# One 512-column matmul for the weights' high part, down projections in two halves of output tiles, and biases written to DRAM once

## The chip, the cores and the metric

The kernel runs on one core of a Trainium2 chip. The metric is device time in microseconds (us) of one execution. The median of three runs of the kernel before is 1639.91 us (1635.03 to 1642.86).

A core has five engines that run their own instruction streams and meet through semaphores: TensorE (PE in the profile; PEld is its loading of weights), VectorE (DVE), ScalarE (ACT), GpSimd (POOL) and SyncE (SP), which here only issues the loads of the weights. Matmul results land in PSUM, in banks of 512 float32 per partition.

## The reference

The reference computes two transformer-like blocks in float32 on one sequence of T = 256 tokens of width D = 1024:

```
def first_block(x, mem, ...):
    mem_n = rmsnorm(mem, mem_norm)
    for l in range(2):
        x = x + 0.5 * swiglu(rmsnorm(x, ffn1_norm[l]), ffn1_w_gate[l], ffn1_w_up[l], ffn1_w_down[l])
        h = rmsnorm(x, mix_norm[l])
        x = x + (even_mixer if l == 0 else odd_mixer)(h, ...)
        x = x + memory_cross_attention(rmsnorm(x, xa_norm[l]), mem_n, ...)
        x = x + 0.5 * swiglu(rmsnorm(x, ffn2_norm[l]), ...)
    return rmsnorm(x, final_norm)
```

`swiglu` is `(silu(x @ w_gate) * (x @ w_up)) @ w_down` with an inner width of 2816 = 22 x 128. `even_mixer` puts a short convolution beside attention in a sliding window of 128 keys (8 heads); `odd_mixer` is causal attention (8 heads) over the whole sequence; both add to the logits a bias that depends on the distance of query and key alone (`rel_bias`, 32 buckets by 8 heads). The cross attention has four heads over a memory of 256 rows. The second block has a swiglu, a mixer of a depthwise convolution beside gated linear attention, another swiglu, and a per-layer embedding with a last norm. There are six swiglus in all.

## The kernel before, in words

**Layout.** Activations lie feature by token: `x` is eight tiles of [128 features, 256 tokens]. Weights come from DRAM in 517 units of [128, 1024] float32 (512 KB), packed on the host in the order of their use. `Builder.unit` (L172) loads one into one of five staging tiles, and `halves` (L151) splits it: ScalarE casts it to `whi` (fp32r, L155), VectorE subtracts to get `wlo` (L158). `wpool` holds eight such pairs. A unit is eight blocks of 128 x 128.

**Products.** Activations are split in the same way, into a high and a low part: `Norm` holds `hh` and `hl` for the normed `x` (`norm_pair`, L309), and `split` (L277) makes `ah` and `al` from an intermediate result. `mm3` (L222) multiplies one block of weights by an operand of 256 columns with three matmuls into the same 256 columns of a bank: high by high (L230), high by low (L231), low by high (L232). `proj` (L241) makes column tiles of a projection, two to a bank of the pool `psw` (four banks); `vproj` (L255) makes a projection by token, with 512 moving columns of weights (L271 to L273).

**Residual sums.** `accumulate` (L287) holds all eight output tiles of a down or output projection in the four banks of the pool `psa`, two tiles to a bank. Each row of weights (a unit: eight blocks) is added to all eight; the last `tail` rows are done pair by pair, and after each pair `updater` (L525) adds the bank to `x` (L530, or L532 with a factor), and `norm_pair` makes the next norm's operands from it (`hh` L316 on ScalarE, L314 on VectorE for the last pair; `hl` L317) and the squares (L328), summed on GpSimd (L336, L339). The norm's factor comes later: its reciprocal roots are spread over the partitions (`rb`) and multiplied into the results of the projection.

**Swiglu.** `ffn` (L401) projects gate and up of tile j into one bank, three tiles ahead (`LAG`) of the down product that uses them: VectorE multiplies the bank by `rb` (L408), ScalarE takes silu (L410), VectorE multiplies gate by up (L412), and `split` gives the operand (L282, L283). Operands live in the pool `act`, eight pairs. The first projection after a norm runs over the tiles of `x` in the outer loop (`kouter`), so that it can begin when the first tiles are normed.

**Attention.** `by_distance` (L599) makes the biases by distance, 8 heads by 384 distances, and writes each of two such tables to DRAM 128 times over (`fd`, [128, 8, 384], L605); `bias_tile` (L480) reads it back along diagonals into `tb`, 128 queries by 256 keys for four heads, which `softmax_block` (L433) adds to the scores (L445).

**Order.** The instructions are traced in program order, and a scheduler that plans with its own cost model orders them on each engine; at run time each engine's stream is in order. Some steps are put off by hand: `b.after` counts blocks of products, `b.bg` runs small steps with each unit of weights, and `HOLD`, `HOLD2` and `ASET` make the splitting of some units wait for a norm's last instructions. Tile pools that open in a stage reuse the memory of pools that have closed, and the first writer waits for the last reader.

The last mixer (`_gla_mixer`, L932) and the embedding at the end use the same helpers.

Of the kernel before, what the change touches and what calls it, by code (L numbers as in the profile page):

```python
# [19 lines left out]
P = 128  # L20
# [7 lines left out]
# swiglu tiles projected ahead of their use, and down tiles whose products end pair by pair  # L28
LAG, TAIL = 3, 3
# [19 lines left out]
# columns of the per-partition parameter array  # L49
# [15 lines left out]
class Norm:  # L65
    """Gained activations split in two, and the reciprocal root mean squares, which come later:
    `finish` gives them by token and a function that spreads them over the partitions."""

    def __init__(self, b, hh, hl, finish):
        self.b, self.hh, self.hl, self.finish = b, hh, hl, finish  # L70
        self.f32 = None
        self.sq = [None, None]
        self.state = 0
        self.gap = 12
        self.waiting = []

    def __call__(self, k):
        return self.hh[:, k, :], self.hl[:, k, :], self.f32 and self.f32[:, k, :]
# [43 lines left out]
class Builder:  # L122
    def __init__(self, ctx, tc, wflat):
# [7 lines left out]
        self.spread = self.square = None  # L131
        e = ctx.enter_context
        self.cpool = e(tc.tile_pool(name="cpool", bufs=1))
        self.stage = e(tc.tile_pool(name="stage", bufs=5))
        self.wpool = e(tc.tile_pool(name="wpool", bufs=8))
        self.work = e(tc.tile_pool(name="work", bufs=2))
        self.small = e(tc.tile_pool(name="small", bufs=4))
        self.act = e(tc.tile_pool(name="act", bufs=8))
# [33 lines left out]
    def unit(self, *slabs, raw=False):  # L172
        """The next 1024 columns of weights, split in two unless `raw`."""
# [10 lines left out]
    def first_units(self, specs, x, x_in, n, g):  # L184
        """The first two units and the input, in pieces that arrive together."""
# [36 lines left out]
    def mm3(self, ps, w, b, a, first, last):  # L222
        """One block of weights by an operand of 256 columns, each the sum of two exact parts."""
# [3 lines left out]
        if raw is not None:  # L227
            mm(ps, raw[:, s], a[2], start=first, stop=last, skip_group_check=True)  # L228
        else:
            mm(ps, hi[:, s], a[0], start=first, stop=False, skip_group_check=True)  # L230
            mm(ps, hi[:, s], a[1], start=False, stop=False, skip_group_check=True)  # L231
            mm(ps, lo[:, s], a[0], start=False, stop=last, skip_group_check=True)  # L232
# [8 lines left out]
    def proj(self, units, h, kouter=False, pool=None):  # L241
        """Column tiles of a projection, two to a bank."""
# [11 lines left out]

    def vproj(self, name, l, c0, h, raw=False):  # L255
        """Token-major projection onto 512 columns: two banks of 128 tokens."""
        banks = [self.psw.tile([P, 512], F32, tag="bank", name="bank") for _ in range(2)]
        mm = self.nc.tensor.matmul
        for u in range(ND // 2):
            hi, lo, w = self.vunit(name, l, u, c0, raw)  # L260
            for kk in range(2):
                k = 2 * u + kk
                ah, al, a = h(k)
# [12 lines left out]

    def split(self, src, name="a"):  # L277
        """A [128, 256] operand as two halves whose sum is exact."""
        nc = self.nc
        ah = self.act.tile([P, T], F32R, tag="ah", name="ah")  # L280
        al = self.act.tile([P, T], F32R, tag="al", name="al")
        nc.scalar.copy(ah, src)  # L282
        nc.vector.tensor_tensor(al, src, ah.bitcast(F32), op=ALU.subtract)  # L283
        return ah, al, None

# [1 line left out]
    def accumulate(self, parts, finish, tail=2):  # L287
        """parts: callables giving (weights, operand); finish(pair, bank)."""
# [15 lines left out]
    def norm_begin(self, finish=None):  # L304
        hh = self.hpool.tile([P, ND, T], F32R, tag="hh", name="hh")
        hl = self.hpool.tile([P, ND, T], F32R, tag="hl", name="hl")
        return Norm(self, hh, hl, finish or self.norm_end)

    def norm_pair(self, n, p, x, g, squares=True):  # L309
        """The operands from two tiles of x, [128, 8, 256], with gains g, [128, 8]."""  # L310
        nc = self.nc
        for d in (2 * p, 2 * p + 1):
            if p == 3:
                nc.vector.tensor_scalar_mul(n.hh[:, d, :], x[:, d, :], g[:, d:d + 1])  # L314
            else:
                nc.scalar.mul(n.hh[:, d, :], x[:, d, :], g[:, d:d + 1])  # L316
            self.last = nc.vector.scalar_tensor_tensor(n.hl[:, d, :], x[:, d, :], g[:, d:d + 1],  # L317
# [954 lines left out]
```

## Time and profile before

| | before |
|---|---|
| median of three runs | 1639.91 us (1635.03 to 1642.86) |
| profiled execution, span from first to last instruction | 1638.6 us |
| granted TensorE clock, mean | 0.987 |
| TensorE busy | 1597.3 us, 97%, 12606 matmuls |
| VectorE busy | 1079.8 us, 66% |
| ScalarE busy | 785.5 us, 48% |
| GpSimd busy | 108.2 us, 7% |
| DMA | 282.68 MB, mean 173 GB/s |

The profile gives no time of its own for the profiled execution beside its span. Engines work side by side, so the busy times don't add up. In a row of a group of instructions stand the line, the engine, the operation, what it writes and reads, the shape and the count; then the busy time and the mean of one; then the idle time of the engine before these instructions and what ended it. A matmul's duration includes the depth of its pipeline; matmuls start closer together than they last.

### The profile page before, as it was taken

What the parts mean: (1) busy time and instruction counts of PE and PEld (TensorE: products, weight loads), DVE (VectorE), ACT (ScalarE), POOL (GpSimd) and SP (SyncE); (2) the same over time, 40 slices, a digit from 0 to 9 for tenths busy, and PEclk for the clock granted to TensorE, in tenths of its full rate; (3) what the DMA queues carried; (4) which work ended last, traced back from release to release, by engine and by line L of the source; (5) the groups of instructions that cost most, each with busy time, mean ns of one, the idle gap of its engine ahead of it and who ended that gap; (6) DMA issues with size and microseconds to landing.
All of it is one profiled execution on the core that took longest, in us unless ns stands there. A gap on an engine that the chain in (4) does not pass through costs nothing. (4 is left out here: it accounts for less than half of the span.)

```text
span 1638.6 us, 30481 instructions
## 1 busy us (share of the span) xinstructions
PE 1597.3 (97%) x12606; PEld 1552.8 (95%) x12606; DVE 1079.8 (66%) x1552; ACT 785.5 (48%) x1201; POOL 108.2 (7%) x133
## 2 busy tenths in 40 slices
PE   8998899999999999999999999999999999999997
PEld 7998798989999999999999999999999978999996
DVE  6744578577656585556856865568555698756556
ACT  6432444355444454444644644454444666544444
POOL 4100010001000000001010100010000100200001
PEclk9999799999999999999999999999999999999999
DMA  7765745264655365553625655536555424665541
GB/s 267 229 165 133 217 169 170 91 206 155 210 186 184 129 231 182 184 186 119 218 78 181 208 191 180 182 115 231 184 187 184 150 84 132 208 205 183 181 142 65
DMA packets 78987, 282.68 MB, mean 173 GB/s; under 512 B 9450, under 2 KB 9722, under 8 KB 78848
## 3 DMA queue, kind: packets, MB, share of 16 engines
q1 hardware_dynamic: 75600, 272.66, 50.2%
q0 software_dynamic: 2672, 7.21, 2.6%
q8 instruction: 99, 1.62, 0.4%
q10 hardware_dynamic: 576, 0.86, 0.2%
q14 instruction: 40, 0.33, 0.1%
HBM read 276.49 MB, written 4.19 MB: 171 GB/s over the span
## 5 line engine op out<-in xcount | busy, mean ns | idle before, releaser
L158 DVE TENSOR_TENSOR wlo<-st,whi 128x1024 fp32r<-128x1024 f32 (+1 forms) x511 | 620.9, 1226 | 274.1 <-ACT whi L155 273.0
L155 ACT CAST whi<-st 128x1024 fp32r<-128x1024 f32 (+1 forms) x511 | 527.4, 1043 | 508.6 <-PE bank L231 331.5
L230 PE MATMUL bank<-hh,whi 128*128 128x256 f32 x2520 | 720.6, 286 | 16.4 <-ACT whi L155 14.7
L232 PE MATMUL bank<-hh,wlo 128*128 128x256 f32 x2520 | 718.5, 285 | 1.3 <-DVE wlo L158 0.9
L231 PE MATMUL bank<-hl,whi 128*128 128x256 f32 x2520 | 718.2, 285 | 0.6 <-DVE hl L317 0.6
L230 PEld LDWEIGHTS bank<-hh,whi 128*128 128x128 f32 x2520 | 488.5, 194 | 19.0 <-ACT whi L155 15.2
L232 PEld LDWEIGHTS bank<-hh,wlo 128*128 128x128 f32 x2520 | 488.2, 194 | 3.0 <-DVE wlo L158 3.0
L231 PEld LDWEIGHTS bank<-hl,whi 128*128 128x128 f32 x2520 | 488.5, 194 | 1.2 <-DVE hl L317 0.8
L230 PE MATMUL abank<-ah,whi 128*128 128x256 f32 x1312 | 372.8, 285 | 1.9 <-ACT whi L155 1.9
L232 PE MATMUL abank<-ah,wlo 128*128 128x256 f32 x1312 | 372.2, 284 | 0.7 <-DVE wlo L158 0.7
L231 PE MATMUL abank<-al,whi 128*128 128x256 f32 x1312 | 372.3, 284 | 0.0
L230 PEld LDWEIGHTS abank<-ah,whi 128*128 128x128 f32 x1312 | 252.6, 193 | 2.9 <-ACT whi L155 2.1
L231 PEld LDWEIGHTS abank<-al,whi 128*128 128x128 f32 x1312 | 252.8, 193 | 1.8 <-issue 1.6
L232 PEld LDWEIGHTS abank<-ah,wlo 128*128 128x128 f32 x1312 | 252.6, 193 | 1.3 <-DVE wlo L158 1.0
L408 DVE TENSOR_TENSOR gu<-bank,rb 128x512 f32<-128x512 f32 x132 | 90.5, 689 | 82.2 <-PE bank L232 82.1
L282 ACT CAST ah<-a 128x256 fp32r<-128x256 f32 x132 | 53.0, 405 | 131.3 <-DVE a L412 131.1
L283 DVE TENSOR_TENSOR al<-a,ah 128x256 fp32r<-128x256 f32 x132 | 56.6, 433 | 52.2 <-ACT ah L282 52.1
L336 POOL TENSOR_TENSOR sqa<-sq 128x256 f32<-128x256 f32 x13 | 10.3, 794 | 1131.6 <-ACT sq L328 953.5
L410 ACT ACTIVATE sg<-gu 128x256 f32<-128x256 f32 x132 | 54.0, 413 | 46.4 <-DVE gu L408 46.3
L339 POOL TENSOR_TENSOR sqa<-sqa,sq 128x256 f32<-128x256 f32 x78 | 69.1, 886 | 35.2 <-ACT sq L328 31.0
L317 DVE SCALAR_TENSOR_TENSOR hl<-x,pc,hh 128x256 fp32r<-128x256 f32 x88 | 57.6, 694 | 12.1 <-ACT hh L316 12.1
L316 ACT ACTIVATE hh<-x,pc 128x256 fp32r<-128x256 f32 x66 | 29.9, 501 | 68.1 <-DVE x L530 41.9
(247 smaller groups left out, 966.6 us busy)
## 6 DMA issues: line engine op xcount, KB each, us to landing
st<-wflat SPq DMA_DIRECT2D x515, 512.0 KB, 4.2
fd<-fs POOLq DMA_DIRECT2D x2, 1536.0 KB, 37.5
tb<-fd POOLq DMA_DIRECT2D x4, 512.0 KB, 4.4
x<-x_in SPq DMA_DIRECT2D x4, 256.0 KB, 5.7
st<-wflat SPq DMA_DIRECT2D x4, 256.0 KB, 5.2
mem<-mem_in POOLq DMA_DIRECT2D x4, 256.0 KB, 8.8
gf<-last_gain POOLq DMA_DIRECT2D x1, 512.0 KB, 8.1
out_dram<-y ACTq DMA_DIRECT2D x2, 256.0 KB, 2.5
```

The source lines that it names most:

```text
L155: self.nc.scalar.copy(w[0][:, s], st[:, s])
L158: self.nc.vector.tensor_tensor(w[1][:, s], st[:, s], w[0][:, s].bitcast(F32), op=ALU.subtract)
L230: mm(ps, hi[:, s], a[0], start=first, stop=False, skip_group_check=True)
L231: mm(ps, hi[:, s], a[1], start=False, stop=False, skip_group_check=True)
L232: mm(ps, lo[:, s], a[0], start=False, stop=last, skip_group_check=True)
L282: nc.scalar.copy(ah, src)
L283: nc.vector.tensor_tensor(al, src, ah.bitcast(F32), op=ALU.subtract)
L316: nc.scalar.mul(n.hh[:, d, :], x[:, d, :], g[:, d:d + 1])
L317: self.last = nc.vector.scalar_tensor_tensor(n.hl[:, d, :], x[:, d, :], g[:, d:d + 1], n.hh[:, d, :].bitcast(F32), op0=ALU.mult, op1=ALU.s ...
L339: add(n.sq[which], n.sq[which], dst[:, e, :], op=ALU.add)
L408: nc.vector.tensor_tensor(gu, bank, self.rb2(n), op=ALU.mult)
L410: nc.scalar.activation(sg, gu[:, 0, :], AF.Silu)
```

## The change

**Operands.** High and low parts of an activation now lie next to each other: `Norm` holds one tile `h2` [128, 8, 2, 256], and `split` makes one tile `a2` [128, 2, 256]. The pool for `a2` is opened per stage (`acts`): 22 in a swiglu, 8 in a mixer, 4 in a cross attention, 2 in the embedding.

**Products.** `mmw` multiplies a block's `wlo` by the high part (256 columns) and its `whi` by both parts (512 columns) into a whole bank; the result is the sum of the bank's two halves. `projw` uses one bank per column tile; ScalarE copies one half out and VectorE adds the other, in a new tile `sum`, which the multiplication by `rb` then reads. It replaces `proj` in the swiglus, both mixers of the first block and the cross attentions. The last mixer keeps `proj`, `mm3`, `accumulate` and the old `updater`; `vproj` stays.

**Residual sums.** `accumulatew` does output tiles 0 to 3 first, row by row, in `psa`, and then 4 to 7 one after the other, in `psw`, each over all rows. `blocks` gives it weights in units of eight blocks in that order, so the number of units stays 517. `updaterw` adds both halves of a bank to `x` in two instructions per output tile, and makes the norm's operands tile by tile.

**Biases.** The tables are written once each ([8, 384]) with the distances in the opposite order; `bias_tile` reads them with a step of one element from partition to partition, and `softmax_block` reads `tb` backward.

**Buffers.** `wpool` has seven pairs in place of eight. `LAG` stays 3; `TAIL` goes.

```diff
+    def blocks(self, order):
+        for i in range(0, len(order), 8):
+            u = self.unit(*order[i:i + 8])
+            for c in range(len(order[i:i + 8])):
+                yield u, c
...
+    def mmw(self, bank, w, b, a, first, last):
+        hi, lo, _ = w
+        s = slice(b * P, (b + 1) * P)
+        a = a[0]
+        mm = self.nc.tensor.matmul
+        mm(bank[:, 0, :], lo[:, s], a[:, 0, :], start=first, stop=False, skip_group_check=True)
+        mm(bank, hi[:, s], a, start=False, stop=last, skip_group_check=True)
+        self.tick()
...
+    def projw(self, units, h, kouter=False):
+        banks = [None] * len(units)
+        sums = []
+        order = [(c, k) for c in range(len(units)) for k in range(ND)]
+        if kouter:
+            order.sort(key=lambda ck: ck[1])
+        for c, k in order:
+            if k == 0:
+                banks[c] = self.psw.tile([P, 2, T], F32, tag="bank", name="bank")
+            self.mmw(banks[c], units[c], k, h(k), first=(k == 0), last=(k == ND - 1))
+            if k == ND - 1:
+                if c % 2 == 0:
+                    sums.append(self.work.tile([P, 2, T], F32, tag="sum", name="sum", bufs=4))
+                dst = sums[-1][:, c % 2, :]
+                self.nc.scalar.copy(dst, banks[c][:, 1, :])
+                self.nc.vector.tensor_tensor(dst, banks[c][:, 0, :], dst, op=ALU.add)
+        return sums
...
+        a = self.act.tile([P, 2, T], F32R, tag="a2", name="a2")
+        nc.scalar.copy(a[:, 0, :], src)
+        nc.vector.tensor_tensor(a[:, 1, :], src, a[:, 0, :].bitcast(F32), op=ALU.subtract)
...
+    def accumulatew(self, name, l, rows, operand, finish):
+        n = len(rows)
+        cols = [slice(d * P, (d + 1) * P) for d in range(ND)]
+        order = [(name, l, r, cols[d]) for r in rows for d in range(4)]
+        blocks = self.blocks(order)
+        banks = None
+        for i in range(n):
+            a = operand(i)
+            if banks is None:
+                banks = [self.psa.tile([P, 2, T], F32, tag="abank", name="abank") for _ in range(4)]
+            for d in range(4):
+                self.mmw(banks[d], *next(blocks), a, first=(i == 0), last=(i == n - 1))
+                if i == n - 1:
+                    finish(d, banks[d])
+        blocks = self.blocks([(name, l, r, cols[d]) for d in range(4, ND) for r in rows])
+        for d in range(4, ND):
+            bank = self.psw.tile([P, 2, T], F32, tag="bank", name="bank")
+            for i in range(n):
+                self.mmw(bank, *next(blocks), operand(i), first=(i == 0), last=(i == n - 1))
+            finish(d, bank)
...
+    def updaterw(n, g, scale=1.0):
+        def f(d, bank):
+            for e in range(2):
+                nc.vector.scalar_tensor_tensor(x[:, d, :], bank[:, e, :], scale, x[:, d, :], op0=ALU.mult, op1=ALU.add)
+            b.norm_tile(n, d, x, g)
+            if d >= 6:
+                b.sq_tile(n, d, x)
+            elif d % 2:
+                b.sq_pair(n, d // 2, x, 0)
...
-        def act(j, bank):
-            gu = self.work.tile([P, 2, T], F32, tag="gu", name="gu")
-            nc.vector.tensor_tensor(gu, bank, self.rb2(n), op=ALU.mult)
+        def act(j, gu):
+            nc.vector.tensor_tensor(gu, gu, self.rb2(n), op=ALU.mult)
...
-        blocks = ((0, slice(0, P), slice(P, T)), (1, slice(P, 384), slice(0, T)))
+        blocks = ((0, slice(0, P), slice(P - 1, None, -1)), (1, slice(P, 384), slice(None, None, -1)))
...
-        src = bass.AP(tensor=f.tensor, offset=f.offset + 127 + 4 * g * 384, ap=[[3071, P], [384, 4], [1, T]])
+        src = bass.AP(tensor=f.tensor, offset=f.offset + 4 * g * 384, ap=[[1, P], [384, 4], [1, T]])
...
-                fd = b.dram.tile([P, 8, 384], F32, tag=f"fd{i}", name="fd")
-                nc.gpsimd.dma_start(fd.rearrange("q h u -> h q u"), fs.unsqueeze(1).to_broadcast([8, P, 384]))
+                fd = b.dram.tile([8, 384], F32, tag=f"fd{i}", name="fd")
+                nc.gpsimd.dma_start(fd, fs)
```

`norm_tile` is the body of `norm_pair` for one tile; `sq_tile` squares one tile and adds it to the sum.

More of the change, by code (lines that the diff above doesn't have):

```diff
@@ L27 @@
 N_UNITS = 517
-LAG, TAIL = 3, 3
+LAG = 3
 HOLD, HOLD2, ASET = 0b11000, 0b100000, 0b10000
@@ L77, in __call__ @@
     def __call__(self, k):
-        return self.hh[:, k, :], self.hl[:, k, :], self.f32 and self.f32[:, k, :]
+        return self.h2[:, k, :, :], self.f32 and self.f32[:, k, :]
     def close(self, wait=0, gap=None):
@@ L275, in vproj, with acts @@
         return banks
+    @contextmanager
+    def acts(self, n):
+        self.n_acts += 1
+        with self.tc.tile_pool(name=f"act{self.n_acts}", bufs=n) as self.act:
+            yield
     def split(self, src, name="a"):
         nc = self.nc
[L280 to L284, printed above, removed]
+        a = self.act.tile([P, 2, T], F32R, tag="a2", name="a2")
+        nc.scalar.copy(a[:, 0, :], src)
+        nc.vector.tensor_tensor(a[:, 1, :], src, a[:, 0, :].bitcast(F32), op=ALU.subtract)
+        return a, None
     def accumulate(self, parts, finish, tail=2):
@@ new lines, in norm_begin, with norm_tile @@
+    def norm_begin(self, finish=None):
+        h2 = self.hpool.tile([P, ND, 2, T], F32R, tag="h2", name="h2")
+        return Norm(self, h2, finish or self.norm_end)
+    def norm_tile(self, n, d, x, g):
+        nc = self.nc
+        hh, hl = n.h2[:, d, 0, :], n.h2[:, d, 1, :]
+        if d >= 6:
+            nc.vector.tensor_scalar_mul(hh, x[:, d, :], g[:, d:d + 1])
+        else:
+            nc.scalar.mul(hh, x[:, d, :], g[:, d:d + 1])
+        self.last = nc.vector.scalar_tensor_tensor(hl, x[:, d, :], g[:, d:d + 1], hh.bitcast(F32),
+                                                   op0=ALU.mult, op1=ALU.subtract)
+        self.since = 0
@@ L309, in norm_pair @@
     def norm_pair(self, n, p, x, g, squares=True):
-        nc = self.nc
         for d in (2 * p, 2 * p + 1):
[L313 to L317, printed above, removed]
-                                                       n.hh[:, d, :].bitcast(F32), op0=ALU.mult, op1=ALU.subtract)
-            self.since = 0
+            self.norm_tile(n, d, x, g)
@@ L398, in rb2, with ffn, swiglu @@
         return n.rb.unsqueeze(1).to_broadcast([P, w, T])
-    def ffn(self, n, gate, up, down, finish, first=None):
+    def ffn(self, n, *args, **kw):
+        with self.acts(NFF):
+            self.swiglu(n, *args, **kw)
+    def swiglu(self, n, gate, up, down, finish, first=None):
         nc = self.nc
@@ L419, in produce, with operand @@
             us = first(specs) if first and j == 0 else [self.unit(*sp) for sp in specs]
-            bank = self.proj(us, n, kouter=(j == 0))[0]
-            n.then(lambda: act(j, bank))
-        def part(j):
-            def f():
-                while nxt[0] < min(j + 1 + LAG, NFF):
-                    produce()
-                return self.rowunit(down[0], down[1], slice(j * P, (j + 1) * P)), acts[j]
-            return f
-        self.accumulate([part(j) for j in range(NFF)], finish, TAIL)
+            s = self.projw(us, n, kouter=(j == 0))[0]
+            n.then(lambda: act(j, s))
+        def operand(j):
+            while nxt[0] < min(j + 1 + LAG, NFF):
+                produce()
+            return acts[j]
+        self.accumulatew(*down, [slice(j * P, (j + 1) * P) for j in range(NFF)], operand, finish)
     def softmax_block(self, heads, score, tb, s, sink=None):
@@ L681, in even @@
                 for i in (0, 2):
-                    bank = b.proj([b.colunit("ev_w_in", 0, qcols[i + e]) for e in range(2)], n)[0]
+                    bank = b.projw([b.colunit("ev_w_in", 0, qcols[i + e]) for e in range(2)], n)[0]
                     nc.vector.scalar_tensor_tensor(q[:, i:i + 2, :], bank, 0.125, b.rb2(n), op0=ALU.mult, op1=ALU.mult)
@@ L746, in even @@
                 rows = [slice(i * P, (i + 1) * P) for i in range(4)] + _permuted_heads(512)
-                b.accumulate([(lambda i=i: (b.rowunit("ev_w_out", 0, rows[i]), ys[i])) for i in range(8)],
-                             updater(n2, mid("xa_norm", 0)))
+                b.accumulatew("ev_w_out", 0, rows, lambda i: ys[i], updaterw(n2, mid("xa_norm", 0)))
         def odd(n, n2):
-            with tc.tile_pool(name="od", bufs=1) as op:
+            with b.acts(8), tc.tile_pool(name="od", bufs=1) as op:
                 tb = b.bias_tile(op, 1, 0)
@@ L858, in products @@
             s = slice(t * P, (t + 1) * P)
-            mm(bank, h[0][:, s], w[0][:, c], start=first, stop=False)
-            mm(bank, h[0][:, s], w[1][:, c], start=False, stop=False)
-            mm(bank, h[1][:, s], w[0][:, c], start=False, stop=last)
+            ah, al = h[0][:, 0, s], h[0][:, 1, s]
+            mm(bank, ah, w[0][:, c], start=first, stop=False)
+            mm(bank, ah, w[1][:, c], start=False, stop=False)
+            mm(bank, al, w[0][:, c], start=False, stop=last)
             b.tick(2)
@@ L958, in conv_in @@
         def conv_in(i, bank):
-            t = b.work.tile([P, 2, T], F32, tag="gu", name="gu")
+            t = b.work.tile([P, 2, T], F32, tag="sum", bufs=4, name="gu")
             nc.vector.tensor_tensor(t, bank, b.rb2(n), op=ALU.mult)
```

88 lines of the change are left out of this document (44 added, 44 removed).

## The prediction

> **What bounds the kernel now.** I read the page's totals first, then the chain, then busy time by stage. In the stage rows the fields after the window are its length, then PE, PEld, DVE, ACT and POOL busy time with the number of instructions, the granted clock, the DMA share and GB/s.
>
> ```profile
> PE 1597.3 (97%) x12606; PEld 1552.8 (95%) x12606; DVE 1079.8 (66%) x1552; ACT 785.5 (48%) x1201; POOL 108.2 (7%) x133
> PE 29%; ACT 1%; DVE 1%; POOL 0%; issue 0%; DMA 0%; POOLq 0%; ACTq 0%; DVEq 0%
> 130.00:140.00 10.00, 10.00 (x86) 10.00 (x86) 4.34 (x11) 3.15 (x6) 0.73 (x1) 1.00 0.01 2
> 158.00:184.00 26.00, 14.17 (x67) 12.60 (x67) 5.57 (x6) 5.83 (x7) 0.00 (x0) 0.68 0.61 138
> 190.00:200.00 10.00, 10.00 (x86) 10.00 (x85) 8.00 (x12) 6.09 (x9) 0.00 (x0) 1.00 0.89 296
> 229.00:250.00 21.00, 19.95 (x158) 19.14 (x157) 19.43 (x29) 11.57 (x12) 3.73 (x5) 0.98 0.77 267
> 330.00:386.00 56.00, 54.85 (x383) 50.71 (x381) 38.41 (x60) 27.70 (x50) 5.89 (x9) 1.00 0.49 160
> 386.00:566.00 180.00, 179.86 (x1498) 179.54 (x1497) 113.46 (x137) 83.48 (x111) 2.07 (x3) 1.00 0.59 194
> ```
>
> TensorE sets the pace: it is busy 97% of the span, and in a swiglu (386 to 566 us) never idle, one matmul per 180 / 1498 = 0.120 us, while VectorE works 63% and ScalarE 46% of it. Two stages are different. From 158 to 184 us only 67 matmuls start; at 0.120 us they need 8.0 us, so 18.0 us are lost. From 229 to 250 us, the head of the first mixer, VectorE works 19.4 of 21 us.
>
> ```profile
> 165.34 1.04 ACT L155 CAST whi<-st 128x1024 fp32r<-128x1024 f32 x1 [18.42 <-DMA st<-wflat]
> 141.80 1.13 POOL L605 DMA_DIRECT2D fd<-fs  x1 [8.18 <-DVE fs L603]
> fd<-fs POOLq DMA_DIRECT2D x2, 1536.0 KB, 37.5
> tb<-fd POOLq DMA_DIRECT2D x4, 512.0 KB, 4.4
> 231.36 0.81 POOL L486 DMA_DIRECT2D tb<-fd  x1
> L445 DVE TENSOR_TENSOR s<-abank,tb x32: 277/352/416, 249.0 to 805.4; 128x128 f32<-128x128 f32 x16, 128x256 f32<-128x256 f32 x16
> st<-wflat SPq DMA_DIRECT2D x515, 512.0 KB, 4.2
> ```
>
> The lost time has its cause here: the second write of the biases (1.5 MB, issued at 141.8, 37.5 us to land, so until about 179) shares the DMA engines with the weights, and ScalarE waits 18.4 us for a unit.
>
> **Term 1, TensorE.** The stage before the end runs the split products with 512 and then with 256 moving columns, each matmul with its own weight load. First of the 512, first and last of the 256:
>
> ```profile
> 1619.71 0.39 PE L859 MATMUL bank<-whi,hh 128*128 128x512 f32 x1
> 1624.47 0.28 PE L859 MATMUL bank<-whi,hh 128*128 128x256 f32 x1
> 1630.10 0.28 PE L861 MATMUL bank<-whi,hl 128*128 128x256 f32 x1
> L230 PE MATMUL bank<-hh,whi 128*128 128x256 f32 x2520 | 720.6, 286 | 16.4 <-ACT whi L155 14.7 <-DVE rb L389 1.7
> L230 PE MATMUL abank<-ah,whi 128*128 128x256 f32 x1312 | 372.8, 285 | 1.9 <-ACT whi L155 1.9
> L230 PE MATMUL bank<-mh,whi 128*128 128x256 f32 x64 | 18.4, 288 | 0.0
> ```
>
> 21 starts lie between the first two rows: 4.76 / 21 = 0.2267 us. 47 lie between the last two: 5.63 / 47 = 0.1198 us. The busy mean of 285 ns is the pipeline's depth and not the price; the price is start to start, 13 ns plus 0.417 ns a column. A block of weights costs 3 x 0.120 = 0.360 us now and 0.120 + 0.2267 = 0.3467 us after: one fixed 13.3 ns is saved. There are 2520 + 1312 + 64 = 3896 blocks. The last mixer keeps the old form for 168 of them (13 units of eight and its 64 output blocks), so 3728 change: 3728 x 13.3 ns = **49.6 us**. The order 256 after 512 in one stream of pairs isn't shown but once (at 1624.47); bounds are no gain (0.360 stays) and 49.6, and I take 49.6, since both widths show the same fixed part.
>
> The Trainium skill, "TensorE: Matmul & The Clock Gate", section "Back-to-back issue gap", speaks against this: it gives an isolated gap of N/2.4 + 2.5 ns, by which a block would go from 327.5 to 325.0 ns and the whole gain would be 9.3 us. The rows give 119.8 and 226.7 where that rule has 109.2 and 215.8, so here a matmul with its load keeps about 13 ns of its own, and the sum goes by the rows.
>
> **Term 2, the biases.** The two writes of 1.5 MB become 12 KB each, and the weights have the engines to themselves. The stall at 158 us goes: **18.0 us**. Bounds: 0 (something else holds the weights back at that point) and 18.0; I take all, since the write's 141.8 to 179 us is where the weights are late. The reads `tb<-fd` keep their 512 KB in 512 rows of 1 KB, now from one 12 KB region; they are issued at 231 us and first used at 249, so 4.4 us may become four times as long at no cost. Weights: 512 KB per eight blocks is 189 GB/s, below the 296 of the row at 190 us.
>
> **Term 3, what the wide bank adds.** Each projected column tile gives two halves: ScalarE copies one out, VectorE adds the other. There are 264 such tiles in the swiglus, 18 in the first mixer, 12 in the second, 16 in the cross attentions: 310. Every residual update becomes two VectorE instructions per output tile where one served a pair.
>
> ```profile
> L158 DVE TENSOR_TENSOR wlo<-st,whi 128x1024 fp32r<-128x1024 f32 (+1 forms) x511 | 620.9, 1226 | 274.1 <-ACT whi L155 273.0
> L155 ACT CAST whi<-st 128x1024 fp32r<-128x1024 f32 (+1 forms) x511 | 527.4, 1043 | 508.6 <-PE bank L231 331.5 <-DMA st<-wflat 132.5 <-issue 15.9
> L408 DVE TENSOR_TENSOR gu<-bank,rb 128x512 f32<-128x512 f32 x132 | 90.5, 689 | 82.2 <-PE bank L232 82.1
> L412 DVE TENSOR_TENSOR a<-sg,gu 128x256 f32<-128x256 f32 x132 | 55.5, 424 | 9.6 <-ACT sg L410 9.6
> L283 DVE TENSOR_TENSOR al<-a,ah 128x256 fp32r<-128x256 f32 x132 | 56.6, 433 | 52.2 <-ACT ah L282 52.1
> L283 DVE TENSOR_TENSOR al<-bank,ah 128x256 fp32r<-128x256 f32 x20 | 8.4, 423 | 9.8 <-ACT ah L282 9.8
> L410 ACT ACTIVATE sg<-gu 128x256 f32<-128x256 f32 x132 | 54.0, 413 | 46.4 <-DVE gu L408 46.3
> L282 ACT CAST ah<-a 128x256 fp32r<-128x256 f32 x132 | 53.0, 405 | 131.3 <-DVE a L412 131.1
> L476 ACT COPY pt<-bank 128x256 f32<-128x256 f32 x16 | 5.5, 373 | 3.9 <-PE bank L475 3.9
> L532 DVE SCALAR_TENSOR_TENSOR x<-abank,x 128x512 f32<-128x512 f32 x24 | 16.5, 688 | 14.3 <-PE abank L232 14.2
> L317 DVE SCALAR_TENSOR_TENSOR hl<-x,pc,hh x88: 468/485/1034, 5.0 to 1602.5; 128x256 fp32r<-128x256 f32 x88
> L314 DVE TENSOR_SCALAR hh<-x,pc x22: 347/353/834, 10.7 to 1600.8; 128x256 fp32r<-128x256 f32 x22
> ```
>
> The copy is L476's 0.373 us, the add L283's from PSUM, 0.423: 116 us on ScalarE (785 to 901) and 131 on VectorE. The half-width update isn't shown; it lies between half of L532 (0.344) and L532 (0.688), and I take 0.423, the PSUM operation of its width. That is 8 x 2 x 0.423 - 4 x 0.688 = 4.0 us for each of ten residual sums, 40 in all: VectorE 1080 + 131 + 40 = 1251, 79% of the new span. What hides it is TensorE. Take a swiglu's first half, where a step is one gate and one up tile and four down blocks: 20 blocks x 0.3467 = 6.93 us. VectorE has 2.5 splits (3.07), two adds (0.85) and L408, L412, L283 (1.55): 5.46 us, 79%. ScalarE has 2.5 casts (2.61), two copies (0.75) and 0.82: 4.17 us. Both fit, and the 331.5 us that casts waited for matmuls to free a weight buffer say that units are split as early as the buffers allow; seven buffers are 19 us ahead, against 4.2 for a landing. The new wait is the add's for the copy: behind it on VectorE stand the multiplication by the norm and the next split, and TensorE misses that split only when the seven buffers are used up. A column tile now holds a whole bank of four, but it is wanted again only four tiles later, 11 us and more.
>
> Where the cover is thin:
> - The last operand of a swiglu is needed 12 blocks (4.2 us) after its projection, where its chain is 0.37 + 0.42 + 0.69 + 0.41 + 0.42 + 0.41 + 0.43 = 3.2 us clean, and may queue behind a split of 1.2. Between 0 and 1 us, six times; I take 0.5 each, **+3**.
> - The cross attention's output product has only four rows, 32 blocks, 11.1 us. Its first output tile is ready after 13 blocks (4.5 us); from there VectorE has eight tiles of two updates (0.85) and `hl` (0.48 to 1.03 by L317's spread; 0.74 taken), and two `hh`: 13.4 us, to 17.9. TensorE is through, with the 14 blocks of the next projection that need no eighth tile, at 11.1 + 4.9 = 16.0, and waits about 1.9 us, twice: **+4** (0 to 10).
> - The first mixer's head, where VectorE has 1.6 of 21 us to spare, gets six adds (2.5 us), its rest 12 more (5.1): **+3** (0 to 13). The upper end is all 18 adds, 7.6 us, and the 16 bias sums (L445, 0.35) at twice their time, 5.6 us, because they now read backward, which no row shows; I take nothing for that.
> - `pin`, the embedding's input:
>
> ```profile
> L850 POOL DMA_DIRECT2D pin<-p_in x1: 629/629/629, 1396.2 to 1396.2; - x1
> DMA to landing us min/median/max: 6.0/6.0/6.0
> ```
>
>   It was loaded at 1396 us, 200 us ahead of use. Its place can now be that of the swiglu's operands, which live until the last output tile, so its issue on the POOL queue may wait until 6.9 us before the end of the swiglu; it lands 6.0 us later and is split in 0.8. Queued behind it on POOL are `gf` and the power of the last norm. 0 to 4 us; **+1.5**.
>
> The ends of the six swiglus I cost at nothing: an output tile there takes 22 blocks, 7.6 us, and its update and split take 2 us.
>
> **The sum** is made against the profiled span: 1638.6 - 49.6 - 18.0 + 3 + 4 + 3 + 1.5 = 1582.5 us. The median of the runs, 1639.9, lies 1.3 above that span, so **1584 us**.
>
> **Rivals.**
> - *VectorE becomes the bound of the swiglus, and the kernel is slower.* Place: the 132 steps. VectorE waits in order for its partners:
>
> ```profile
> DVE gu L408 <- PE bank L232: 82.1, 92, 3.4
> DVE al L283 <- ACT ah L282: 62.1, 124, 2.0
> DVE a L412 <- ACT sg L410: 9.6, 15, 2.1
> ```
>
>   Per step that is 0.62 + 0.47 + 0.07, and two adds that wait for their copies like `al` for `ah` make 0.94 more: 2.1 us. If no split fills these waits a step takes 5.46 + 2.1 = 7.56 us, 0.63 over TensorE's, and 132 x 0.63 = 83 us bring it to 1667. It decides from waits of 1.47 us a step; from 1.90 the kernel is slower than before. Against it: today's waits stand beside idle time, and with 1.2 us splits ready they are filled. 7%.
> - *The short stages cost more.* First mixer +13, the cross attentions +10, the second mixer with its 12 adds +5, pin +4, the last operands +6 in place of 11.5: 1638.6 - 67.6 + 38 + 1.3 = 1610. For it speaks the row at 229 us; against it the 69% of VectorE in the stage of a cross attention (330 to 386 us). Between 1596 and 1615, 16%.
> - *The stall stays,* because the queue of weights was already empty before the write began (DMA 0.01 from 130 to 140 us): +18, 1602. Against it: TensorE ran on for another 17 us after the write was issued, on what was split, and 17 us are six units. 6%.
> - *The wide matmul saves nothing:* the mixed pair keeps 0.360 us, and only the biases gain: 1638.6 - 18 + 11.5 + 1.3 = 1633. By the page's fixed part it would be 1624. The 68 starts above speak against both. 5%.
> - *None of the small costs appears,* and TensorE starts sooner after each norm since output tiles end one by one: below 1570. 6%.
>
> **How the numbers follow.** The forecast itself has 60%, from 1570 (no small cost: 1638.6 - 67.6 + 1.3 = 1572) to 1596. With the next two cases down to 1566 and up to 1612 the range holds a little over 8 in 10. A change under 0.5% (8.2 us) can't be told from none: 1632 is its upper edge for faster. Faster: 0.60 + 0.16 + 0.06 + 0.06 and 0.02 of the wide matmul's 0.05, 0.90. Same: its other 0.03 and 0.01 of VectorE's 0.07. Slower: 0.06.
>
> **What would show it.** After: pairs of starts 0.120 and 0.227 us apart, 0.347 a block; the page's DMA without the 1.5 MB writes and 158 to 184 us full; VectorE near 1250 and ScalarE near 900 us; swiglu steps of 6.9 us with no TensorE idle. I am wrong if VectorE or ScalarE releases TensorE in the middle of a swiglu, if the copies or adds come out above 0.5 us, if TensorE waits for `hl` or `x` for more than 3 us behind a cross attention, or if gaps that start with a late weight landing remain.

## The result and the profile after

The changed kernel takes 1571.76 us (median; runs from 1570.51 to 1573.09), against 1638.11 for the kernel before in the same series: ratio 0.960, 95% interval 0.958 to 0.962. The forecast of 1584 is 12 us high; the range holds the time, and so does the likeliest case's own range (1570 to 1596). The profiled span is 1571.0 us, against 1582.5 in the sum.

The page after: the span, the busy times, the chain's shares, and the bias reads among the DMA issues (KB each, then us to landing).

```profile
span 1571.0 us, 23505 instructions
PE 1541.8 (98%) x8878; PEld 1339.5 (85%) x8878; DVE 1215.3 (77%) x1982; ACT 880.3 (56%) x1521; POOL 126.0 (8%) x133
PE 30%; DVE 1%; ACT 1%; issue 0%; POOL 0%; DMA 0%; POOLq 0%; ACTq 0%
tb<-fd POOLq DMA_DIRECT2D x4, 512.0 KB, 4.2
```

TensorE still sets the pace, with 3728 matmuls fewer. Busy time by stretch, columns as in the prediction's stage rows:

```profile
158.00:184.00 26.00, 26.00 (x152) 22.91 (x151) 18.47 (x30) 13.54 (x22) 4.02 (x3) 1.00 0.37 118
201.00:222.00 21.00, 20.35 (x119) 17.29 (x117) 17.78 (x31) 12.09 (x17) 1.53 (x2) 1.00 0.70 232
336.00:352.00 16.00, 16.00 (x94) 14.11 (x93) 11.74 (x29) 7.67 (x15) 5.49 (x7) 1.00 0.00 1
540.00:700.00 160.00, 160.00 (x926) 141.13 (x925) 123.04 (x184) 90.10 (x150) 4.03 (x3) 1.00 0.59 188
1360.00:1520.00 160.00, 160.00 (x907) 138.69 (x906) 120.29 (x178) 89.33 (x149) 7.22 (x5) 1.00 0.57 184
```

The stall at 158 us is gone. The head of the first mixer (now 201 to 222) and the end of the cross attention (336 to 352) are nearly full or full. Both swiglu rows have no idle TensorE, yet the second holds 907 matmuls where the first holds 926. The order of TensorE's starts tells why (start, duration):

```profile
420.10 0.28 PE L250 MATMUL bank<-h,wlo 128*128 128x256 f32 x1
420.22 0.39 PE L251 MATMUL bank<-h,whi 128*128 128x512 f32 x1
...
421.83 0.28 PE L250 MATMUL bank<-h,wlo 128*128 128x256 f32 x1
...
1420.10 0.28 PE L250 MATMUL bank<-h,wlo 128*128 128x256 f32 x1
1420.22 0.40 PE L251 MATMUL bank<-h,whi 128*128 128x512 f32 x1
...
1421.87 0.28 PE L250 MATMUL abank<-a,wlo 128*128 128x256 f32 x1
```

Five blocks take 1.73 us in the first place, 0.346 each, as predicted, and 1.77 us in the second, 0.354, at the same granted clock of 1.00 and with no wait. I call these the quick and the long rhythm. Over all consecutive pairs of the profile (3628 of 3728 blocks; worked out from the starts) the mean is 0.3486 us, 1.9 ns above the quick one.

Groups by line (count, then busy time, mean ns; idle time before them):

```profile
L251 PE MATMUL bank<-h,whi 128*128 128x512 f32 x2416 | 851.4, 394 | 0.0
L250 PE MATMUL bank<-h,wlo 128*128 128x256 f32 x2416 | 681.1, 282 | 9.8 <-DVE wlo L158 9.8
L158 DVE TENSOR_TENSOR wlo<-st,whi 128x1024 fp32r<-128x1024 f32 (+1 forms) x511 | 630.2, 1254 | 63.8 <-ACT whi L155 63.5
L289 ACT COPY sum<-bank 128x256 f32<-128x256 f32 x310 | 114.1, 370 | 262.1 <-PE bank L251 261.9
L290 DVE TENSOR_TENSOR sum<-bank,sum 128x256 f32<-128x256 f32 x310 | 130.2, 422 | 115.2 <-ACT sum L289 114.7
```

The 310 copies and adds cost what the sum took (0.373 and 0.423 us). TensorE waited for a split 9.8 us in the whole run, while VectorE's idle time ahead of a split fell from 274.1 to 63.8 us: the adds and halved updates were largely paid from that.

### The profile page after: what moved, and what is told of

The parts are those of the page before. It is cut to its first block, busy times and chain, and to the rows that moved or that the text cites. A ratio compares the mean times of both kernels' runs of the same rounds, so it can differ in the third digit from the quotient of the medians.

```text
span 1571.0 us, 23505 instructions
## 1 busy us (share of the span) xinstructions
PE 1541.8 (98%) x8878; PEld 1339.5 (85%) x8878; DVE 1215.3 (77%) x1982; ACT 880.3 (56%) x1521; POOL 126.0 (8%) x133
## 5 line engine op out<-in xcount | busy, mean ns | idle before, releaser
L251 PE MATMUL bank<-h,whi 128*128 128x512 f32 x2416 | 851.4, 394 | 0.0
L250 PE MATMUL bank<-h,wlo 128*128 128x256 f32 x2416 | 681.1, 282 | 9.8 <-DVE wlo L158 9.8
L158 DVE TENSOR_TENSOR wlo<-st,whi 128x1024 fp32r<-128x1024 f32 (+1 forms) x511 | 630.2, 1254 | 63.8 <-ACT whi L155 63.5
L251 PEld LDWEIGHTS bank<-h,whi 128*128 128x128 f32 x2416 | 453.7, 188 | 103.1 <-DVE h L384 0.5
L250 PEld LDWEIGHTS bank<-h,wlo 128*128 128x128 f32 x2416 | 457.7, 189 | 13.5 <-DVE wlo L158 8.4
L251 PE MATMUL abank<-a,whi 128*128 128x512 f32 x624 | 222.9, 393 | 0.0
L290 DVE TENSOR_TENSOR sum<-bank,sum 128x256 f32<-128x256 f32 x310 | 130.2, 422 | 115.2 <-ACT sum L289 114.7
L251 PE MATMUL bank<-a,whi 128*128 128x512 f32 x624 | 218.1, 393 | 0.0
L250 PE MATMUL abank<-a,wlo 128*128 128x256 f32 x624 | 176.1, 282 | 0.2 <-DVE wlo L158 0.2
L250 PE MATMUL bank<-a,wlo 128*128 128x256 f32 x624 | 175.1, 281 | 0.0
L250 PEld LDWEIGHTS bank<-a,wlo 128*128 128x128 f32 x624 | 117.9, 189 | 0.0
```

What stands on the lines that cost most here:

```text
L158: self.nc.vector.tensor_tensor(w[1][:, s], st[:, s], w[0][:, s].bitcast(F32), op=ALU.subtract)
L250: mm(bank[:, 0, :], lo[:, s], a[:, 0, :], start=first, stop=False, skip_group_check=True)
L251: mm(bank, hi[:, s], a, start=False, stop=last, skip_group_check=True)
L290: self.nc.vector.tensor_tensor(dst, banks[c][:, 0, :], dst, op=ALU.add)
```

## The experiments

Times are medians; the kernel before took 1639.08, 1638.78 and 1636.03 us in the three series, and ratios are to it. Stage lengths are worked out from matmul starts between the residual updates.

**The parts one by one.** First the biases alone, in the kernel before:

```diff
-        blocks = ((0, slice(0, P), slice(P, T)), (1, slice(P, 384), slice(0, T)))
+        blocks = ((0, slice(0, P), slice(P - 1, None, -1)), (1, slice(P, 384), slice(None, None, -1)))
...
-                fd = b.dram.tile([P, 8, 384], F32, tag=f"fd{i}", name="fd")
-                nc.gpsimd.dma_start(fd.rearrange("q h u -> h q u"), fs.unsqueeze(1).to_broadcast([8, P, 384]))
+                fd = b.dram.tile([8, 384], F32, tag=f"fd{i}", name="fd")
+                nc.gpsimd.dma_start(fd, fs)
...
```

> The kernel before with the bias tables written once and read backward, and nothing else of the change. Theory (the two terms are separate, and the writes of 1.5 MB starve the weights at 158 us): the 26 us from 158 to 184 us run full, 18 us less, 1638.1 - 18 = 1620 us (1616 to 1624). Rival (the weights were late there for another reason, or the small reads clash): within 4 us of 1638.

1616.44 us, ratio 0.987 [0.985, 0.990]; span 1614.2. The stretch of the stall, in this kernel:

```profile
158.00:184.00 26.00, 26.00 (x219) 26.00 (x219) 15.51 (x19) 11.30 (x15) 0.00 (x0) 1.00 0.55 184
```

219 matmuls stand where 67 stood: 152 x 0.120 = 18.2 us at this place, the predicted term. The whole gain is 22.6 us by the medians and 24.4 by the spans. Of the spans' difference 22.9 us lie in the first swiglu and 2.3 in the first mixer and cross attention behind it. In the swiglu 3.1 us beside the stall are in the first 40 us, ahead of any bias write (before, then here):

```profile
0.00:20.00 20.00, 11.87 (x63) 10.71 (x64) 11.69 (x21) 13.49 (x21) 8.47 (x14) 0.93 0.78 279
20.00:40.00 20.00, 20.00 (x155) 20.00 (x154) 15.69 (x21) 12.43 (x22) 7.59 (x9) 0.90 0.79 257
```

```profile
0.00:20.00 20.00, 12.80 (x75) 11.88 (x76) 12.10 (x22) 13.62 (x21) 9.00 (x15) 1.00 0.78 279
20.00:40.00 20.00, 20.00 (x169) 20.00 (x168) 16.18 (x21) 13.42 (x23) 7.81 (x9) 1.00 0.83 271
```

26 matmuls more, at a granted clock of 1.00 in place of 0.93 and 0.90. Nothing here shows that the edit has to do with that clock, and the kernel before varies with it by itself: its runs of this series go from 1631.38 us at a mean granted clock of 0.993 to 1641.67 at 0.986, where the four runs of the edit stand at 1615.27 to 1617.78 and 0.996 to 0.997. So the 4 to 6 us of gain beyond the stall aren't shown to be the edit's.

Second, the changed kernel with each 512-column matmul split in two:

```diff
-        mm(bank, hi[:, s], a, start=False, stop=last, skip_group_check=True)
+        mm(bank[:, 0, :], hi[:, s], a[:, 0, :], start=False, stop=last, skip_group_check=True)
+        mm(bank[:, 1, :], hi[:, s], a[:, 1, :], start=False, stop=last, skip_group_check=True)
```

> The changed kernel with the 512-column matmul in two of 256 columns, everything else kept: copies, adds, halves of output tiles, biases. Theory (only the fixed 13.3 ns of a matmul with its load is saved): starts 0.120 us apart again, 3728 x 13.3 ns = 49.6 us more, 1571.8 + 49.6 = 1621 us (1617 to 1626), equal to the kernel before with the biases alone. Rival (part of the gain comes from the new order of output tiles and the smaller PSUM tiles): 1595 to 1615. Rival (the rearrangement costs time, hidden by the wide matmul's gain): above 1630.

1612.06 us, ratio 0.985 [0.982, 0.988]; span 1612.4. TensorE's starts:

```profile
420.02 0.28 PE L250 MATMUL abank<-a,wlo 128*128 128x256 f32 x1
...
421.46 0.28 PE L250 MATMUL bank<-h,wlo 128*128 128x256 f32 x1
```

Twelve matmuls in 1.44 us: 0.120 us each, here and in every swiglu. So the wide matmul itself is worth 1612.06 - 1571.76 = 40.3 us (41.4 by the spans; 36 to 39 by the medians that the changed kernel had in the later series). Everything else in the change (halved output tiles, copies and adds, seven buffers, the later load of `pin`) stands between the two experiments: -4.4 us by the medians, -1.8 by the spans, where the prediction had +11.5. The spans close: 1638.6 - 24.4 - 1.8 - 41.4 = 1571.0.

Third, the 1.5 MB writes put back into the changed kernel:

```diff
...
-                fd = b.dram.tile([8, 384], F32, tag=f"fd{i}", name="fd")
-                nc.gpsimd.dma_start(fd, fs)
+                fd = b.dram.tile([P, 8, 384], F32, tag=f"fd{i}", name="fd")
+                nc.gpsimd.dma_start(fd.rearrange("q h u -> h q u"), fs.unsqueeze(1).to_broadcast([8, P, 384]))
...
```

The distances and the reads go back to their old form with it.

> The changed kernel with the biases written 128 times over and read forward along diagonals, as before. Theory: the stall comes back, 1571.8 + 18 = 1590 us (1584 to 1594). It could be larger, since TensorE now uses a unit in 2.78 us instead of 2.88 and the split buffers are seven instead of eight: 37.5 us of write at the same share leave one unit less, up to 5 us more. Rival (the stall came from the old order of splits around it, with 0.01 of DMA from 130 to 140 us): within 4 us of 1572.

1612.52 us, ratio 0.985 [0.982, 0.988]: 40.8 us more than the changed kernel, over twice the expected 18. Waits from 95 to 200 us, then two windows:

```profile
ACT whi L155 <- DMA st<-wflat: 51.7, 10, 10.8
```

```profile
100.00:110.00 10.00, 4.90 (x25) 4.07 (x24) 3.33 (x6) 2.04 (x4) 0.00 (x0) 0.93 0.66 136
160.00:170.00 10.00, 3.37 (x17) 2.74 (x16) 2.58 (x4) 1.62 (x3) 0.00 (x0) 0.83 0.60 115
```

```profile
75.39 1.13 POOL L692 DMA_DIRECT2D fd<-fs  x1 [27.19 <-DVE fs L690]
143.49 1.13 POOL L692 DMA_DIRECT2D fd<-fs  x1 [9.34 <-DVE fs L690]
```

Both writes starve the weights here. The first does so from 103 us on; in the kernel before it was issued at 77 us as well, and TensorE ran through it, on units that had been split earlier (VectorE, third busy time, makes two instructions in this stretch):

```profile
100.00:110.00 10.00, 10.00 (x85) 10.00 (x85) 1.72 (x2) 2.09 (x2) 0.00 (x0) 1.00 0.68 137
```

Two guesses at why the stock doesn't last here were followed.

*The seven buffers.* The kernel before, with one buffer pair less:

```diff
-        self.wpool = e(tc.tile_pool(name="wpool", bufs=8))
+        self.wpool = e(tc.tile_pool(name="wpool", bufs=7))
```

> The kernel before with seven pairs of split weight buffers in place of eight, as the changed kernel has. It tells why the repeated bias writes cost 41 us in the changed kernel and 22 in the old one. Theory (one unit less of split weights is most of it): the stall at 158 us begins a unit earlier and the first write, landing at 115 us, begins to show: 1645 to 1658 us. Rival (it is the changed kernel's quicker use of units and its other order of splits): 1638 to 1643, one unit of 2.88 us at most.

1630.65 us, ratio 0.996 [0.994, 0.998]: 5 us faster, not slower. The stall begins as before, near 157 us; its rows here:

```profile
160.00:170.00 10.00, 4.87 (x21) 4.58 (x22) 1.23 (x1) 1.04 (x1) 0.00 (x0) 0.55 0.59 112
```

The gain lies in the first mixer (4.4 us), the first swiglu (2.4, most of it the start's clock) and the last (2.1). Neither expectation allowed for it, and its cause is not settled. *Fewer units split ahead:* at 75 us 4.8 units are split and not yet used in the third experiment, 6.2 in the kernel before (worked out from the traces). Both have split 27 units by then; the difference is on TensorE, which has used 178 blocks in the one and 166 in the other, in whose first 40 us the granted clock was lower. VectorE is busy for all of 40 to 60 us in both kernels, and from 60 to 75 us for 13.3 of 15 us in the third experiment and 9.9 in the kernel before, so the changed kernel has less room to catch up. But no run varied the stock by itself, so why the undoing costs 41 us and the doing brings 24 stays open.

**The add on VectorE.** The changed kernel without it; this leaves out the bank's first half, the products with the activation's high part, so each projected tile lacks the main part of its sum and the time is that of less work:

```diff
-                self.nc.vector.tensor_tensor(dst, banks[c][:, 0, :], dst, op=ALU.add)
```

> The changed kernel without VectorE's add of the bank's first half in the wide projections: the low half of each projected tile's sum is left out, the copy stays. 310 x 0.42 = 130 us of VectorE work go. Theory (hidden under TensorE in the swiglus and, as the trace now says, in the mixers too): 0 to 3 us less, 1569 to 1572 us. Rival (the adds cost what the prediction took for the first mixer and the last operands): 5 us or more less, below 1567.

1564.79 us, ratio 0.956 [0.953, 0.960]: 7.0 us less, the rival's time and not the 0 to 3 us of the theory, though still little for 110 us of VectorE's work (1215.3 to 1105.1). Of the span's 9.2 us, 3.4 are the long rhythm, which the last swiglu doesn't show here; the two mixers of the first blocks give 2.2, the cross attentions 1.4, the fifth swiglu 1.7 (some 0.5 of it a piece in the long rhythm). The second, third and fourth swiglu are unchanged to 0.1 us. So the adds cost 4 to 6 us, most of it in short stages.

**How near the bound is.** Two, then four more VectorE instructions per projected tile, which change nothing in the result (a maximum of the tile with itself). First the changed kernel once more, in the same series:

> The changed kernel once more, beside the next one on the same chip: 1570 to 1574 us.

1575.75 us, ratio 0.962 [0.960, 0.965].

```diff
                 self.nc.vector.tensor_tensor(dst, banks[c][:, 0, :], dst, op=ALU.add)
+                self.nc.vector.tensor_tensor(dst, dst, dst, op=ALU.max)
+                self.nc.vector.tensor_tensor(dst, dst, dst, op=ALU.max)
```

> The changed kernel with two further VectorE instructions per projected tile, each the maximum of the sum with itself, so that only work is added: 4 x 0.42 = 1.69 us per swiglu step, 5.53 + 1.69 = 7.22 us against 6.94 of TensorE. Theory (VectorE's in-order waits are filled by splits, and the limit is its busy time): 0.28 x 22 = 6.2 us per swiglu are owed, which the split buffers (seven units, 8.6 us of VectorE) can lend; 0 to 15 us more with the mixers, 1572 to 1587. Rival (the waits aren't filled, the changed kernel already stands at the edge): a step takes 7.22 and 1.2 of waits, 1.5 us x 132 = 195 us more.

1599.79 us, ratio 0.977 [0.973, 0.979]: 24 us more than the changed kernel beside it, between the 15 of the one theory and the 195 of the other: neither holds it, and it is much nearer the first.

Waits of VectorE from 540 to 700 us, in the changed kernel and then here (total, times, longest):

```profile
DVE sum L290 <- ACT sum L289: 18.9, 36, 2.3
```

```profile
DVE sum L290 <- ACT sum L289: 2.9, 3, 1.8
```

```profile
540.00:700.00 160.00, 158.61 (x917) 138.56 (x916) 146.84 (x266) 87.01 (x146) 3.44 (x4) 1.00 0.59 197
```

VectorE now works 146.8 of 160 us, its waits have shrunk, and TensorE is still busy for 158.6. The extra 24 us lie mostly at the start: 8.4 in the first swiglu, 5.7 in the first mixer, 1.7 to 3.9 in each of the next four swiglus (against the changed kernel's first profile). The 3.9 are those of the second, which here runs mostly in the long rhythm.

```diff
                 self.nc.vector.tensor_tensor(dst, banks[c][:, 0, :], dst, op=ALU.add)
+                self.nc.vector.tensor_tensor(dst, dst, dst, op=ALU.max)
+                self.nc.vector.tensor_tensor(dst, dst, dst, op=ALU.max)
+                self.nc.vector.tensor_tensor(dst, dst, dst, op=ALU.max)
+                self.nc.vector.tensor_tensor(dst, dst, dst, op=ALU.max)
```

> The same with four further instructions per projected tile: 3.38 us per step, 8.91 us of VectorE against 6.94. Theory: 1.97 x 22 = 43 us per swiglu, less 8.6 of lent splits, is 35, six times 208 us, and 10 to 30 in the mixers: 1790 to 1810 us. Rival (waits not filled): above 1900.

1819.53 us, ratio 1.111 [1.107, 1.114]: 10 us above the theory's range, and 80 below the rival's 1900. A wait of TensorE from 420 to 580 us, inside the second swiglu, and the row of this stretch:

```profile
PE bank L250 <- DVE wlo L158: 10.7, 7, 3.1
420.00:580.00 160.00, 147.14 (x807) 126.06 (x806) 152.99 (x320) 80.58 (x135) 0.71 (x1) 0.97 0.49 162
```

The changed kernel has no wait of TensorE in this stretch. So the limit lies between two and four more operations a tile. At 0.335 us from start to start (measured below) they bring a step's 5.46 us on VectorE to an estimated 6.80 and 8.14, either side of TensorE's 6.93. Here the later steps of the second to the sixth swiglu take 7.9 to 8.2 us (from one multiplication by `rb` to the next), and VectorE works 153.0 of these 160 us and waits 6.7: its work decides, and not its waits.

**The load of `pin`.** It and `gf` get a pool of their own, ahead of the last swiglu:

```diff
+    ip = ctx.enter_context(tc.tile_pool(name="ip", bufs=1))
+    pin = ip.tile([P, 2, T], F32, tag="pin", name="pin")
+    nc.gpsimd.dma_start(pin, p_in)
+    gf = ip.tile([P, D], F32, tag="gf", name="gf")
+    nc.gpsimd.dma_start(gf, last_gain.partition_broadcast(P))
...
-        pin = pp.tile([P, 2, T], F32, tag="pin", name="pin")
-        nc.gpsimd.dma_start(pin, p_in)
-        gf = pp.tile([P, D], F32, tag="gf", name="gf")
-        nc.gpsimd.dma_start(gf, last_gain.partition_broadcast(P))
```

> The changed kernel with the embedding's input and last gain in a pool of their own, opened ahead of the last swiglu, so that their loads don't wait for the swiglu's operands. Theory (the 2.9 us without a matmul start after the last swiglu come from this load, which the trace shows issued at 1529.0 us, after the last matmul's start at 1528.3): 2 to 4 us less, 1568 to 1570 us. Rival (TensorE waits there for the squares of the last output tile anyway): within 1 us of the changed kernel.

1570.55 us, ratio 0.958 [0.956, 0.960], span 1575.8. From the start of the last swiglu's last matmul to the kernel's last one it takes 30.8 us, as in the kernel before (30.8); the changed kernel's three profiles have 34.2, 33.0 and 34.2. So the late load costs 2.2 to 3.4 us there. The whole span doesn't show it, since two other swiglus of this one profile run in the long rhythm: 229 matmuls from 400 to 440 us, where the changed kernel has 233:

```profile
400.00:440.00 40.00, 40.00 (x229) 34.72 (x228) 29.07 (x43) 22.00 (x37) 0.00 (x0) 1.00 0.55 186
```

**The order of the two matmuls.** The 512-column one first:

```diff
-        mm(bank[:, 0, :], lo[:, s], a[:, 0, :], start=first, stop=False, skip_group_check=True)
-        mm(bank, hi[:, s], a, start=False, stop=last, skip_group_check=True)
+        mm(bank, hi[:, s], a, start=first, stop=False, skip_group_check=True)
+        mm(bank[:, 0, :], lo[:, s], a[:, 0, :], start=False, stop=last, skip_group_check=True)
```

> The changed kernel with the 512-column matmul of each block ahead of the 256-column one. The traces of the changed kernel show two rhythms of a block, 0.347 and 0.353 us, that hold for whole swiglus and change from run to run. Theory (the rhythm comes from how the weight load of one falls under the matmul before it, by chance of the start, whatever the order): both rhythms again, 1569 to 1577 us. Rival (the order decides): one rhythm alone, 1566 to 1570 us if it is the quick one, 1590 to 1597 if it is the slow one (3728 x 6.7 ns = 25 us).

1570.43 us, ratio 0.961 [0.959, 0.962], and the changed kernel in the same series:

> The changed kernel once more, beside these on the same chip: 1570 to 1576 us, by how many swiglus run in the slower rhythm (3.5 us each).

1572.93 us, ratio 0.962 [0.960, 0.964]. Two swiglus with the 512-column matmul first; in the second of these stretches the third profile of the changed kernel has 908 matmuls:

```profile
540.00:700.00 160.00, 160.00 (x924) 139.70 (x923) 120.52 (x184) 88.86 (x150) 4.03 (x3) 1.00 0.56 190
1360.00:1520.00 160.00, 160.00 (x923) 139.71 (x922) 118.67 (x180) 90.41 (x150) 6.48 (x5) 1.00 0.56 186
```

With the wide one first no whole swiglu runs in the long rhythm, but the second and the fourth take 183.1 to 183.4 us where those of the changed kernel take 182.6 in the quick rhythm, and 186.4 in the long one. A gain of 2.5 us by the medians is within what the runs scatter. Both edits together:

> The same with the embedding's input and last gain loaded ahead of the last swiglu. Theory (the two edits are in different stages and add up): 3 to 4 us less than the one before it; the stage after the last swiglu 30 us in place of 33 to 34. Rival (the load's wait isn't on the path): no difference beyond 1 us.

1568.84 us (1568.38 to 1569.09), ratio 0.960 [0.958, 0.961]: 4.1 us below the changed kernel in this series, whose runs went from 1569.96 to 1575.06. Against the order alone it is 1.6 us, where 3 to 4 were expected; the end of the kernel, counted as above, falls from 32.9 to 31.2 us, which is 1.7. It is the fastest complete version of the study. TensorE at the end of its last swiglu:

```profile
1527.63 0.28 PE L251 MATMUL bank<-a,wlo 128*128 128x256 f32 x1
1528.40 0.50 PE L946 MATMUL abank<-whi,a 128*128 128x512 f32 x1 [0.49 <-ACT a L327]
```

## Why the prediction held, and where it was off

**Term 1** was 49.6 us and measured 41.4 by the spans. The mechanism is right: one fixed part per block goes, and in the quick rhythm a block costs the 0.347 us of the sum. The step that failed is "both widths show the same fixed part": it priced a mixed stream by unmixed ones. In the long rhythm a block keeps half of the 13.3 ns: 3628 blocks at 1.9 ns above the quick one are 7.0 of the 8.2 us. Of the rivals, "saves nothing" fell: it needed 1633 where the first two experiments and the result leave 40 us to the wide matmul. The Trainium skill, "TensorE: Matmul & The Clock Gate", section "Back-to-back issue gap", whose isolated gap would have given 1624, differs from the rows: 109.2 and 215.8 ns by it, 117 and 230 between the quick starts, 120 in the stream of 256 alone. Its figure for a sustained stream at 512 columns, about 131 ns, isn't reached by any row here.

**Term 2** was 18.0 us and measured 24.4 (22.6 by the medians). The stall was sized rightly, 18.2. The rest by the spans is the clock of the first 40 us (3.1, not shown to be the edit's) and small pieces around the stall and behind it. "The stall stays" fell with the full window.

**Term 3** was +11.5 us; the rearrangement without the wide matmul came out at -1.8. Some of that is the seven buffers, which the sum had at nothing: in the kernel before they alone made the first mixer 4.4 and the last swiglu 2.1 us shorter, and from the first experiment to the second these two stages became 4.4 and 2.2 us shorter. If that is the same effect, the rest of the rearrangement costs some 5 us; no run gives the changed kernel its eighth pair back, so it isn't shown. By parts:

- *Last operand of a swiglu, +3:* none seen. The windows of the swiglus are full, and without the adds three of them stayed the same to 0.1 us.
- *Cross attention, +4:* TensorE has no gap; the 16 us window above is full. The failed step is the 13.4 us of VectorE's work, in which durations were added as if nothing overlapped:

```profile
340.70 1.76 DVE L616 SCALAR_TENSOR_TENSOR x<-abank,x 128x256 f32<-128x256 f32 x5 [3.68 <-PE abank L251]
...
350.71 0.91 DVE L384 SCALAR_TENSOR_TENSOR h<-x,pc,h 128x256 fp32r<-128x256 f32 x1
```

  Five updates of 0.42 us take 1.76 us: (1.76 - 0.42) / 4 = 0.335 from start to start. VectorE is through at 351.62, 10.9 us after its first update. For the same reason its busy time is 1215 and not 1251, while the adds' row is the 131 predicted: the page counts overlaps once. Summed by duration VectorE's work grew from 1146 to 1319 us, by 173 where the prediction had 171.
- *First mixer, +3:* the adds cost about 1.4 us there by their removal, the backward reads nothing:

```profile
L524 DVE TENSOR_TENSOR s<-abank,tb x32: 281/354/426, 220.7 to 758.3; 128x128 f32<-128x128 f32 x16, 128x256 f32<-128x256 f32 x16
```

  354 ns at the median, against 352. VectorE's 17.8 of 21 us in the mixer's head are even less than the 19.4 before, so the cover I called thin was thicker than I took it.
- *`pin`, +1.5:* the place was right, and the size, 2.2 to 3.4, lies in the upper half of 0 to 4. First POOL and ScalarE, then TensorE:

```profile
1529.04 0.62 POOL L935 DMA_DIRECT2D pin<-p_in  x1 [4.79 <-PE bank L251]
1529.77 0.42 ACT L416 ACTIVATE sq<-x 128x256 f32<-128x256 f32 x1 [6.53 <-DVE x L616]
1530.34 0.81 POOL L417 TENSOR_TENSOR sqa<-sqa,sq 128x256 f32<-128x256 f32 x1
```

```profile
1528.34 0.40 PE L251 MATMUL bank<-a,whi 128*128 128x512 f32 x1
1531.20 0.61 PE L428 MATMUL bank<-ones,sqa 128*128 128x1 f32 x4 [2.47 <-POOL sqa L417]
1533.00:1536.00 3.00, 3.00 (x10) 2.42 (x9) 3.00 (x6) 2.30 (x3) 1.01 (x1) 0.60 0.79 254
```

  The issue waits until the last matmul of the swiglu is done, not until 6.9 us before it. TensorE then makes no start for 2.87 us, until the last norm's sum of squares is there. The load in front of that sum on POOL doesn't hold it up: it starts 0.15 us after its squares are ready (1529.77 + 0.42 = 1530.19), and with both edits it is 0.15 us too (1529.83 after 1529.26 + 0.42). What is missing is other work: with the load ahead TensorE goes on after 0.77 us with the embedding's own product, while the sum is made (the lines at 1527.63 and 1528.40 above). Here this product comes at 1532.99, and from 1533 to 1536 us the granted clock is 0.60, where it was 1.00 for the product with both edits.

**The rival of VectorE** was weighed rightly. Waits after:

```profile
DVE sum L290 <- ACT sum L289: 114.7, 199, 2.4
DVE a L328 <- ACT a L327: 38.1, 72, 1.4
DVE a L493 <- ACT sg L491: 9.9, 13, 3.8
```

Spread over 132 steps these are (114.7 + 38.1 + 9.9) / 132 = 1.23 us at most, under the 1.47 where it was to decide; and with two more operations a tile the waits shrink, as "with splits ready they are filled" had it. "Short stages cost more" fell with the full windows. "None of the small costs appears" is nearest to what happened in the short stages (all but `pin` and the adds' small part); its time, below 1570, wasn't reached because term 1 fell short.

So three errors offset each other: the wide matmul 8.2 us less, the biases 6.4 more, the rearrangement 13.3 better; together 11.5, the distance from 1582.5 to 1571.0. That the sum came so close is in part luck.

## What to carry to other kernels

Price a matmul by its start-to-start time, and a saving in a mixed stream by a run of that very mix, since the unmixed rows gave a fifth too much here (49.6 for 41.4 us). Take queue times of VectorE from start to start too: durations added one by one made a 4 us wait that wasn't there. A broadcast written to DRAM beside a weight stream costs what it starves, and a load that takes a place freed late can cost the work that would have filled the next wait.

## What was not expected of the hardware

**Two rhythms.** The same alternation of 256 and 512 columns, with a weight load each, runs at 0.347 or at 0.353 us a pair (means of whole swiglus), at full granted clock and without a wait. Once a swiglu has begun in one it mostly stays in it, and its 528 blocks then take 3.5 us more in the long one; which swiglu it is changes between profiles: of the changed kernel's three, the sixth, then the fifth, then both, and the second and third with `pin` loaded early. Pieces of the first swiglu show it each time. The mean pair was 0.3486, 0.3484 and 0.3493 us in the three. With the 512-column matmul first the mean is 0.3474 and 0.3473 in the two profiles. What sets the rhythm isn't settled.

**A 1.5 MB broadcast** from eight partitions takes 37.5 us to land, 1.5 MB / 37.5 us = 42 GB/s, and while it runs the core's whole traffic is 111 to 157 GB/s in stretches of 10 us (the kernel before, the same with seven pairs, and the third experiment), where 296 GB/s were seen without it.

**One buffer pair less** made the kernel before 5 us faster, where a shorter lead could only be expected to cost.
